# Moving six subtractions from GpSimd to VectorE in the first norm of a two-layer model, with an earlier weight load, one reordered subtraction per step and a 32-byte pad less

## The chip, the cores and the metric

The kernel runs on one core of a Trainium2 chip. A time is the device time of one execution in microseconds (us), and a kernel's time is the median of its runs. One further execution was taken under the hardware profiler; all durations of single instructions come from that one.

## The reference

The model has two layers over 512 tokens of width 1024. Each layer is a mixer (layer 0 a gated linear recurrence, layer 1 attention) followed by a mixture of 16384 small experts; each of these four parts is preceded by a norm whose scale and shift come from a vector `c` by a matrix:

```
def ada_modulation(c, w, b):
    mod = jax.nn.silu(c) @ w + b
    shift, scale, gate = jnp.split(mod, 3, axis=-1)

shift, scale, gate = ada_modulation(c, mw, mb)
h = rms_norm(x, g) * (1.0 + scale) + shift
x = x + gate * mixer(h, *mixer_params[layer])
```

The change touches the very first of the four norms and the first products of the mixer behind it (`xb, gb = jnp.split(h @ in_w, 2, axis=-1)`).

## The kernel before, in words

Every large matrix product is made from a split into two float32r halves: `hi` is a rounded copy that ScalarE writes, `lo` is the raw value minus `hi`, a subtraction with two inputs in SBUF. Three TensorE products then stand for one: `hi*hi`, `hi*lo`, `lo*hi`. `split` (lines 226 to 228) does this for weights, with ScalarE on line 227 and, on line 228, VectorE or, while the stream's `on_pool` is set, GpSimd.

`Stream` (line 128) feeds the weights of the whole program in the order in which they are used. `fetch` allocates a raw buffer (two of 1 MB, a block pair each) and issues its load on SyncE's DMA queue, `fill` splits blocks as far as asked, and `take` hands out one block.

`norm_first` (line 231) runs once, at the start of the program. It brings in the four token tiles of `x` and 16 rows of the modulation matrix (`mrow`, 512 KB each, a ring of 10), in the order scale row 8, shift row 0, then 9, 1, 10, 2 and so on; after every few rows it calls `g.stream.fetch()` for a pair of weight blocks. `normed_rows` scales each token tile (the `rs` power is a small GpSimd instruction) and TensorE transposes it into eight PSUM banks, one for each slice `k` of 128 channels. For each `k`:

- two `dot` calls: VectorE multiplies a row with `silu(c)` and sums it (line 278), ScalarE turns the sum into a column (lines 280, 283);
- ScalarE makes `hk = xt * scale + shift` (line 310) and its rounded copy `hhi` (line 311), VectorE subtracts `hlo = hk - hhi` (line 312);
- for `k` of 1 to 4 the next of four weight blocks is taken and split; at `k = 6` two more blocks are split ahead for the mixer;
- `products` issues the TensorE work that has become possible (lines 299 to 301): 4 blocks x 8 slices x 3 products, 96 in all.

Behind the norm, `lru` (line 530) reads the four finished blocks (ScalarE lines 613, 615, 625) and goes on with `proj_t` (lines 423 to 425), whose first PSUM bank is free when the `ge` activation of line 625 has read its block.

Each engine works through its own instructions strictly in the order in which they stand. That order is chosen by the scheduler of the language layer; an instruction wrapped in `tc.keep_in_program_order` keeps its place among others so wrapped. A DMA queue belongs to the engine that issues on it: a DMA that has to wait for a buffer holds up all later ones of the same engine.

Of the kernel before, what the change touches and what calls it, by code (L numbers as in the profile page):

```python
# [18 lines left out]
KD = D // 128  # L19
# [43 lines left out]
def setup(tc, ctx, g, x, c, out):  # L63
# [24 lines left out]
    nc.vector.memset(g.mhalf, -0.5)  # L88
    pad(g, g.const, 32)
    g.order = range(TC)  # L90
# [37 lines left out]
class Stream:  # L128
# [3 lines left out]
    def __init__(self, g, items, ahead=3):  # L132
# [5 lines left out]
        self.on_pool = False  # L138
        self.fetched = 0
        self.spare = None  # L140

    def fetch(self):

        (src, shape, n), b = self.blocks[len(self.parts)]
        self.loads += 1
        raw, bufs = self.g.wraw, 2
        if self.third and self.loads % 3 == 0:
            raw, bufs = self.third
        self.raw = raw.tile([128, n, *shape], F32, name="wraw", tag="wraw", bufs=bufs)
        self.g.nc.sync.dma_start(self.raw, src)  # L150
        self.fetched = self.loads

    def fill(self, last):
# [3 lines left out]
        while len(self.parts) <= last:  # L157
            (src, shape, n), b = self.blocks[len(self.parts)]
            if b == 0:
                if not self.fetched:  # L160
                    self.fetch()
                self.fetched = 0
            raw = self.raw[:, b]
# [67 lines left out]
def norm_first(g, mwT, sub):  # L231
# [8 lines left out]
    with pool(tc, name="mw0", bufs=10) as mw, pool(tc, name="nw", bufs=2) as nw, \  # L240
# [7 lines left out]
        def loads():  # L248
# [8 lines left out]
            for k in range(1, KD):  # L257
                fetch(KD + k)
                fetch(k)
                if k in (2, 4):  # L260
                    yield
                    g.stream.fetch()
# [12 lines left out]
        def dot(r):  # L275
            wf = rows.pop(r).rearrange("p a b -> p (a b)")
            d = nw.tile([128, 1], F32, name="dot", tag="dot", bufs=4)
            V.scalar_tensor_tensor(wf, wf, 1.0, g.sc, op0=OP.mult, op1=OP.mult, accum_out=d)
            if r < KD:
# [22 lines left out]

        for k in range(KD):
            if k:
                dot(KD + k)
                dot(k)
            if k in (1, 3):
                next(moved)
            hk = nw.tile([128, S], F32, name="hk", tag="hk")
            A.activation(hk, xt[k], AF.Identity, scale=cols[KD + k], bias=cols[k])  # L310
            A.activation(hhi[:, k, :], hk, AF.Copy)
            V.tensor_sub(hlo[:, k, :], hk, hhi[:, k, :])
            if 1 <= k <= m:
                g.stream.on_pool = True
                g.stream.spare = nw if k <= 2 else None
                w.append(g.stream.take(0))
                g.stream.on_pool = False
            if k == KD - 2:
                g.stream.on_pool = True
                g.stream.fill(m + 1)  # L320
                g.stream.on_pool = False
            if k:
# [1152 lines left out]
```

## Time and profile before

| | us |
|---|---|
| median of 3 runs | 3165.71 (3160.58 to 3170.85) |
| profiled execution, its own time | 3167.8 |
| its span in the trace | 3166.0 |
| TensorE (PE) busy | 3061.6 |
| VectorE (DVE) busy | 2556.2 |
| ScalarE (ACT) busy | 1468.7 |
| GpSimd (POOL) busy | 1000.5 |

In a line of the timeline view the columns are the start and the duration in us, the engine, the source line, the operation, what it writes and reads, the count of merged instructions, and in brackets the idle time ahead of it and what ended that. SPq is SyncE's DMA queue; PEld is TensorE's weight load. Instructions of one engine overlap a little, so the distance between two starts is what one costs its engine, somewhat less than its duration.

### The profile page before, as it was taken

The numbers are of one execution on the slowest core, as the hardware profiler recorded it, in microseconds if no ns is written. First come the engines' busy times: TensorE is split into PE (matmuls) and PEld (weight loads), VectorE is DVE, ScalarE is ACT, GpSimd is POOL, SyncE is SP. The second block draws the span as 40 slices with busy tenths as digits, with TensorE's granted clock in tenths as the row PEclk, the third lists the DMA queues.
The fourth block names the chain that finished last, engine by engine and source line by source line (L and its number), as shares of the span: only waits on it lengthen the run. The fifth ranks groups of instructions, "written<-read, shape, count | busy, mean of one in ns | idle before, by whom it ended". The sixth has DMA issues, their size and how long they took to land.

```text
span 3166.0 us, 44376 instructions
## 1 busy us (share of the span) xinstructions
PE 3061.6 (97%) x16192; PEld 2686.4 (85%) x16192; DVE 2556.2 (81%) x5260; ACT 1468.7 (46%) x2129; POOL 1000.5 (32%) x859
## 2 busy tenths in 40 slices
PE   6998999999999999999899999999999999999999
PEld 5876999998788888888777778999987888888887
DVE  7866779977988888887579976789968888888884
ACT  5763337873333333333458744257853333333332
POOL 3001540007545246552011103420036454544430
PEclk9998999999999999999999999999999999999999
DMA  6545344789999999997332243345799999999983
GB/s 262 167 174 168 114 146 145 271 295 393 370 372 349 376 358 357 363 351 264 125 118 94 82 147 119 121 148 212 270 353 384 353 371 336 350 335 350 355 314 117
DMA packets 304780, 818.98 MB, mean 259 GB/s; under 512 B 27824, under 2 KB 156848, under 8 KB 276016
## 3 DMA queue, kind: packets, MB, share of 16 engines
q1 hardware_dynamic: 173680, 391.93, 35.5%
q0 software_dynamic: 89408, 321.43, 27.1%
q10 hardware_dynamic: 41472, 102.78, 8.7%
q8 instruction: 127, 2.08, 0.3%
q14 instruction: 93, 0.76, 0.1%
HBM read 735.03 MB, written 81.02 MB: 258 GB/s over the span
## 4 chain that ended last, share of the span: by engine, by line
PE 71%; DVE 15%; DMA 5%; ACT 4%; issue 4%; POOL 1%; SPq 0%; DVEq 0%; ACTq 0%; POOLq 0%
PE vacc L1038 28%; PE pacc L425 11%; PE pacc L423 11%; PE pacc L424 11%; DVE wlo L228 3%; DVE pg L929 2%; DMA wraw<-in_l_v_dram 2%; DMA wraw<-in_l_uT_dram 1%; DVE rows L953 1%; PE gps L905 1%; DVE p L921 1%; DVE p L918 1%; DVE ge L816 1%; DMA at<-ascr 1%; ACT whi L227 1%
## 5 line engine op out<-in xcount | busy, mean ns | idle before, releaser
L227 ACT ACTIVATE whi<-wraw 128x1024 fp32r<-128x1024 f32 (+2 forms) x646 | 663.3, 1034 | 651.2 <-PE pacc L424 392.3
L423 PE MATMUL pacc<-hhi,whi 128*128 128x384 f32 (+1 forms) x2616 | 922.1, 352 | 10.6 <-ACT whi L227 6.6
L425 PE MATMUL pacc<-hhi,wlo 128*128 128x384 f32 (+1 forms) x2616 | 918.5, 351 | 7.7 <-DVE wlo L228 7.7
L424 PE MATMUL pacc<-hlo,whi 128*128 128x384 f32 (+1 forms) x2616 | 916.9, 350 | 0.0
L228 DVE TENSOR_TENSOR wlo<-wraw,whi 128x1024 fp32r<-128x1024 f32 (+1 forms) x566 | 683.1, 1210 | 184.4 <-ACT whi L227 184.0
L1038 PE MATMUL vacc<-wlo,wh 128*128 128x512 f32 x1536 | 605.8, 394 | 1.1 <-DVE wlo L228 1.1
L1038 PE MATMUL vacc<-whi,wh 128*128 128x512 f32 x1536 | 602.7, 392 | 2.2 <-ACT whi L227 2.2
L1038 PE MATMUL vacc<-whi,wl 128*128 128x512 f32 x1536 | 597.2, 389 | 4.9 <-DVE wl L1031 4.9
L423 PEld LDWEIGHTS pacc<-hhi,whi 128*128 128x128 f32 x2616 | 494.6, 189 | 41.3 <-ACT whi L227 7.4
L425 PEld LDWEIGHTS pacc<-hhi,wlo 128*128 128x128 f32 x2616 | 494.0, 189 | 34.8 <-DVE wlo L228 10.8
L424 PEld LDWEIGHTS pacc<-hlo,whi 128*128 128x128 f32 x2616 | 494.7, 189 | 28.8 <-issue 1.7
L1028 ACT ACTIVATE wh<-at 128x384 fp32r<-128x384 f32 x256 | 134.1, 525 | 790.4 <-DVE at L1024 532.0
L944 POOL DMA_INDIRECT rows<-in_l_v_dram,ei x256 | 361.6, 1412 | 382.4 <-DVE accg L965 342.7
L944 POOL DMA_INDIRECT rows<-in_l_u_dram,ei x256 | 370.8, 1449 | 282.7 <-DVE rows L953 230.6
L1038 PEld LDWEIGHTS vacc<-whi,wl 128*128 128x128 f32 x1536 | 288.7, 188 | 70.5 <-DVE wl L1031 6.1
L1038 PEld LDWEIGHTS vacc<-whi,wh 128*128 128x128 f32 x1536 | 288.6, 188 | 64.2 <-ACT whi L227 2.6
L1038 PEld LDWEIGHTS vacc<-wlo,wh 128*128 128x128 f32 x1536 | 289.0, 188 | 54.2 <-DVE wlo L228 1.8
L965 DVE SCALAR_TENSOR_TENSOR accg<-rows,act,accg 128x1024 f32<-128x1024 f32 x254 | 324.7, 1278 | 0.5
L953 DVE SCALAR_TENSOR_TENSOR rows<-rows,hn 128x1024 f32<-128x1024 f32 x256 | 304.8, 1220 | 15.0 <-DMA rows<-in_l_u_dram,ei 15.0
L1024 DVE TENSOR_TENSOR at<-at,gtile 128x384 f32<-128x384 f32 x256 | 140.9, 553 | 147.7 <-DMA at<-ascr 141.4
L228 POOL TENSOR_TENSOR wlo<-wraw,whi 128x1024 fp32r<-128x1024 f32 (+1 forms) x80 | 171.5, 2155 | 226.9 <-ACT whi L227 226.9
L907 ACT ACTIVATE st<-gps 128x512 f32<-128x512 f32 x192 | 184.5, 1110 | 39.0 <-PE gps L905 38.8
(295 smaller groups left out, 3401.1 us busy)
## 6 DMA issues: line engine op xcount, KB each, us to landing
wraw<-in_l_uT_dram SPq DMA_DIRECT2D x128, 1024.0 KB, 7.0
wraw<-in_l_v_dram SPq DMA_DIRECT2D x128, 1024.0 KB, 9.9
gscr<-st ACTq DMA_DIRECT2D x48, 1024.0 KB, 4.6
gtile<-gscr SPq DMA_DIRECT2D x32, 1536.0 KB, 16.9
mw<-in_l_ffn_mw_dram POOLq DMA_DIRECT2D x48, 512.0 KB, 3.6
ascr<-at ACTq DMA_DIRECT2D x112, 192.0 KB, 2.7
at<-ascr ACTq DMA_DIRECT2D x112, 192.0 KB, 8.3
mw<-in_l_mix_mw_dram POOLq DMA_DIRECT2D x32, 512.0 KB, 6.5
```

The costliest lines, as they stand in the source:

```text
L227: g.nc.scalar.activation(hi, raw, AF.Copy)
L228: (eng or g.nc.vector).tensor_sub(lo, raw, hi)
L423: nc.tensor.matmul(ps, whi[:, k, :], hhi[:, k, :n], start=(k == 0), stop=False)
L424: nc.tensor.matmul(ps, whi[:, k, :], hlo[:, k, :n], start=False, stop=False)
L425: nc.tensor.matmul(ps, wlo[:, k, :], hhi[:, k, :n], start=False, stop=(k == KD - 1))
L907: A.activation(st[:, :, q * 4:q * 4 + 4].rearrange("p e t -> p t e"), gps, AF.Copy, scale=1.0 / GSCALE)
L944: i = nc.gpsimd.indirect_dma_start(out=rows, out_offset=None, in_=src, in_offset=bass.IndirectOffsetOnAxis(ap=ei[:, j:j + 1], axis=0))
L953: V.scalar_tensor_tensor(r, r, 1.0, hn, op0=OP.mult, op1=OP.mult, accum_out=act[:, j:j + 1]))
L965: tc.keep_in_program_order(V.scalar_tensor_tensor(acc, r, w, acc, op0=OP.mult, op1=OP.add))
L1024: pin(V.tensor_tensor(at.rearrange("p (b t) -> p b t", t=16), at.rearrange("p (b t) -> p b t", t=16), gts[c // 8][:, :, c % 8, :], op=OP.m ...
L1028: pin(A.activation(wh, at, AF.Copy))
L1038: T.matmul(acc[t][d], x[:, ts], y[:, d, :], start=(i == 0 and x is wh and y is vh), stop=(i == PK - 1 and x is wl))
```

## The change

Five edits, all in the first norm, its stream helper and the setup:

1. The six low halves of weights that the first norm splits go from GpSimd to VectorE.
2. The two pairs of weight blocks are asked for after modulation rows 1 and 3 instead of 2 and 4. `fetch` may now run ahead of blocks that are not split yet.
3. `finish(k)` issues `hk` and `hhi` and returns the subtraction for `hlo`; it is issued after the dots of slice `k + 1`.
4. The dots and the `hlo` subtractions are kept in program order.
5. A pad of 32 bytes per partition in the constants is removed, with its GpSimd memset. Every tile that is allocated behind it on the left side of SBUF starts 32 bytes lower; the tiles of `x`, on the right side, stay.

```
-    pad(g, g.const, 32)
@@ Stream
-        self.fetched = 0
+        self.next = None
...
-        (src, shape, n), b = self.blocks[len(self.parts)]
+        (src, shape, n), b = next(x for x in self.blocks[len(self.parts):] if x[1] == 0)
...
-        self.raw = raw.tile([128, n, *shape], F32, name="wraw", tag="wraw", bufs=bufs)
-        self.g.nc.sync.dma_start(self.raw, src)
-        self.fetched = self.loads
+        self.next = raw.tile([128, n, *shape], F32, name="wraw", tag="wraw", bufs=bufs)
+        self.g.nc.sync.dma_start(self.next, src)
...
-                if not self.fetched:
+                if self.next is None:
                     self.fetch()
-                self.fetched = 0
+                self.raw, self.next = self.next, None
@@ norm_first
-                if k in (2, 4):
+                if k in (1, 3):
                     yield
                     g.stream.fetch()
...
-            V.scalar_tensor_tensor(wf, wf, 1.0, g.sc, op0=OP.mult, op1=OP.mult, accum_out=d)
+            tc.keep_in_program_order(
+                V.scalar_tensor_tensor(wf, wf, 1.0, g.sc, op0=OP.mult, op1=OP.mult, accum_out=d))
...
-        for k in range(KD):
-            if k:
-                dot(KD + k)
-                dot(k)
-            if k in (1, 3):
-                next(moved)
+        def finish(k):
             hk = nw.tile([128, S], F32, name="hk", tag="hk")
             A.activation(hk, xt[k], AF.Identity, scale=cols[KD + k], bias=cols[k])
             A.activation(hhi[:, k, :], hk, AF.Copy)
-            V.tensor_sub(hlo[:, k, :], hk, hhi[:, k, :])
+            return lambda: tc.keep_in_program_order(V.tensor_sub(hlo[:, k, :], hk, hhi[:, k, :]))
+
+        for k in range(KD):
+            if k in (0, 2):
+                next(moved)
+            low = finish(k)
+            if k + 1 < KD:
+                dot(KD + k + 1)
+                dot(k + 1)
+            low()
             if 1 <= k <= m:
-                g.stream.on_pool = True
                 g.stream.spare = nw if k <= 2 else None
                 w.append(g.stream.take(0))
-                g.stream.on_pool = False
             if k == KD - 2:
-                g.stream.on_pool = True
                 g.stream.fill(m + 1)
-                g.stream.on_pool = False
```

What this makes of the order of instructions is shown at three places. Behind the first norm, the rows of all engines are the same in both programs, apart from line numbers and one load of gate weights on SyncE's queue, which now stands ahead of the three small loads `cv`, `gbias` and `lm` of the mixer, not behind them.

The first place is VectorE from the third token tile's `rs` on (`xn` is a scaled token tile, `mrow,dot` a dot, `wlo` the low half of a weight block). Before:

```order
L344 TENSOR_SCALAR ms<-ss 128x1
L278 SCALAR_TENSOR_TENSOR mrow,dot<-mrow,sc 128x1024
L348 TENSOR_SCALAR xn<-x_199,rs 128x512 x2
L278 SCALAR_TENSOR_TENSOR mrow,dot<-mrow,sc 128x1024 x2
L312 TENSOR_TENSOR hlo<-hk,hhi 128x512 x2
L278 SCALAR_TENSOR_TENSOR mrow,dot<-mrow,sc 128x1024
L312 TENSOR_TENSOR hlo<-hk,hhi 128x512
L278 SCALAR_TENSOR_TENSOR mrow,dot<-mrow,sc 128x1024 x3
```

And in the changed program:

```order
L343 TENSOR_SCALAR ms<-ss 128x1
L347 TENSOR_SCALAR xn<-x_197,rs 128x512 x2
L277 SCALAR_TENSOR_TENSOR mrow,dot<-mrow,sc 128x1024 x2
L306 TENSOR_TENSOR hlo<-hk,hhi 128x512
L226 TENSOR_TENSOR wlo<-wraw,whi 128x1024
L277 SCALAR_TENSOR_TENSOR mrow,dot<-mrow,sc 128x1024 x2
L306 TENSOR_TENSOR hlo<-hk,hhi 128x512
L277 SCALAR_TENSOR_TENSOR mrow,dot<-mrow,sc 128x1024
L226 TENSOR_TENSOR wlo<-wraw,whi 128x1024
```

One dot has moved from ahead of the last token tile to behind it, and the first low half of a weight stands between the first `hlo` and the dots of slice 2.

The second place is VectorE at the end of the first norm. Before:

```order
L278 SCALAR_TENSOR_TENSOR mrow,dot<-mrow,sc 128x1024 x3
L312 TENSOR_TENSOR hlo<-hk,hhi 128x512
L278 SCALAR_TENSOR_TENSOR mrow,dot<-mrow,sc 128x1024 x3
L312 TENSOR_TENSOR hlo<-hk,hhi 128x512 x2
L612 MEMSET xp 128x3 x2
```

And in the changed program:

```order
L277 SCALAR_TENSOR_TENSOR mrow,dot<-mrow,sc 128x1024 x2
L306 TENSOR_TENSOR hlo<-hk,hhi 128x512
L226 TENSOR_TENSOR wlo<-wraw,whi 128x1024 x2
L306 TENSOR_TENSOR hlo<-hk,hhi 128x512
L611 MEMSET xp 128x3 x2
```

The two low halves for the mixer's next blocks now stand ahead of the last `hlo`.

The third place is GpSimd from its constants to the mixer (`mw` is a modulation row that the mixer's background work reads). Before:

```order
L96 IOTA ji 128x128
L56 MEMSET pad 128x8
L96 IOTA ji 128x128
L346 TENSOR_TENSOR rs<-ms,mhalf 128x1 x4
L228 TENSOR_TENSOR wlo<-wraw,whi 128x1024 x6
L185 DMA mw<-in_l_mix_mw_dram 128x1024 x8
```

And in the changed program:

```order
L1470 UNCONDITIONAL_BRANCH
L95 ISA
L95 IOTA ji 128x128 x2
L345 TENSOR_TENSOR rs<-ms,mhalf 128x1 x4
L183 DMA mw<-in_l_mix_mw_dram 128x1024 x8
```

The first `mw` loads stand directly behind the last `rs`; the first two of them wait for nothing else.

## The prediction

> **What bounds the kernel now.** I read the page's busy times and its chain first, then the windows view, to see where TensorE has slack at all.
>
> ```profile
> PE 3061.6 (97%) x16192; PEld 2686.4 (85%) x16192; DVE 2556.2 (81%) x5260; ACT 1468.7 (46%) x2129; POOL 1000.5 (32%) x859
> PE 71%; DVE 15%; DMA 5%; ACT 4%; issue 4%; POOL 1%; SPq 0%; DVEq 0%; ACTq 0%; POOLq 0%
> 0.00:58.00 58.00, 34.09 (x130) 25.17 (x131) 37.24 (x59) 32.27 (x60) 22.69 (x18) 1.00 0.66 253
> 800.00:1200.00 400.00, 394.75 (x1906) 348.22 (x1906) 343.78 (x523) 139.35 (x193) 186.72 (x147) 1.00 0.99 362
> 2500.00:2900.00 400.00, 400.00 (x1945) 353.81 (x1944) 329.21 (x427) 140.69 (x193) 190.88 (x135) 1.00 0.96 349
> ```
>
> In the last three lines the columns are the stretch, its length, the busy time of PE, PEld, DVE, ACT and POOL with counts, the granted clock, the DMA share and GB/s. TensorE works 97% of the span; it is idle for 104 us in all, and 24 of these lie in the first 58 us. This is the stage that the change edits; behind it the order of instructions is the same. So the question is one number: when does TensorE begin the mixer's first own product (line 423), now at 57.58? Whatever that start gains, the PE-bound rest passes on nearly whole.
>
> Next I read the timeline of that stage, engine by engine.
>
> ```profile
> 18.26 1.22 DVE L278 SCALAR_TENSOR_TENSOR mrow<-mrow,sc 128x1024 f32<-128x1024 f32 x1
> 26.37 6.35 POOL L228 TENSOR_TENSOR wlo<-wraw,whi 128x1024 fp32r<-128x1024 f32 x2 [8.94 <-ACT whi L227]
> 27.13 3.36 DVE L278 SCALAR_TENSOR_TENSOR mrow<-mrow,sc 128x1024 f32<-128x1024 f32 x1
> 39.15 3.37 DVE L278 SCALAR_TENSOR_TENSOR mrow<-mrow,sc 128x1024 f32<-128x1024 f32 x1
> 44.82 0.50 PE L301 MATMUL pacc<-hhi,wlo 128*128 128x512 f32 x1 [0.32 <-POOL wlo L228]
> 51.73 0.69 DVE L312 TENSOR_TENSOR hlo<-hk,hhi 128x512 fp32r<-128x512 f32 x1 [1.24 <-ACT hhi L311]
> 54.59 0.39 PE L301 MATMUL pacc<-hhi,wlo 128*128 128x512 f32 x1
> 55.02 0.60 ACT L613 ACTIVATE xp<-pacc 128x512 f32<-128x512 f32 x1 [1.43 <-PE pacc L301]
> 56.65 0.39 PE L301 MATMUL pacc<-hhi,wlo 128*128 128x512 f32 x1
> 56.93 0.60 ACT L625 ACTIVATE ge<-pacc 128x512 f32<-128x512 f32 x1
> 57.58 0.50 PE L423 MATMUL pacc<-hhi,whi 128*128 128x512 f32 x1 [0.54 <-ACT ge L625]
> ```
>
> A dot takes 1.22 us alone; the two shown beside GpSimd's subtractions, and the two that follow them, take 3.4: two-input instructions of the two engines hold each other up. VectorE is done with the last `hlo` at 52.4, but TensorE still works off a backlog until 57.0, because the low half of the fourth block came only at 44.82. So two things end the stage: VectorE's queue, and behind it TensorE's backlog.
>
> **The change, part by part.** *Taken away:* four dots cost 3.37 - 1.22 = 2.15 us less each, 8.6 us of VectorE.
>
> *Added:* six low halves of weights on VectorE. The nearest row is the same instruction in the mixer; the dots' starts show what one of that size costs its engine.
>
> ```profile
> 74.79 1.22 DVE L228 TENSOR_TENSOR wlo<-wraw,whi 128x1024 fp32r<-128x1024 f32 x1
> 45.77 0.68 DVE L312 TENSOR_TENSOR hlo<-hk,hhi 128x512 fp32r<-128x512 f32 x1
> 46.38 1.21 DVE L278 SCALAR_TENSOR_TENSOR mrow<-mrow,sc 128x1024 f32<-128x1024 f32 x1
> 47.52 1.21 DVE L278 SCALAR_TENSOR_TENSOR mrow<-mrow,sc 128x1024 f32<-128x1024 f32 x1
> ```
>
> From 46.38 to 47.52 is 1.14 for a dot, and the same for a low half of a weight; from 45.77 to 46.38 is 0.61 for an `hlo`. Six low halves are 6.8 us.
>
> *Moved dot:* row 9's dot goes behind the last token tile, 1.14 more for later. In return no dot stands beside the second and fourth `rs`.
>
> ```profile
> 9.60 0.57 POOL L346 TENSOR_TENSOR rs<-ms,mhalf 128x1 f32<-128x1 f32 x1 [1.53 <-DVE ms L344]
> 11.29 1.46 POOL L346 TENSOR_TENSOR rs<-ms,mhalf 128x1 f32<-128x1 f32 x1 [1.12 <-DVE ms L344]
> ```
>
> The second shrinks from 1.46 to about 0.57, and the fourth alike. Row 0's dot and the column behind it now stand behind the second token tile and hold up the third tile's squares on ScalarE by about 1.5 us, so I set the start of the dots behind the last tile at 18.26 as before (bounds 17.4, if only the `rs` gain counts, and 19.4).
>
> *New waits:* now VectorE itself waits for ScalarE's `whi`, in order, ahead of its next dots. What ScalarE needs from a dot's end I take from these rows.
>
> ```profile
> 48.67 1.22 DVE L278 SCALAR_TENSOR_TENSOR mrow<-mrow,sc 128x1024 f32<-128x1024 f32 x1
> 50.25 0.78 ACT L310 ACTIVATE hk<-xt,col_l_mix,col_l_mix 128x512 f32<-128x512 f32 x1
> 51.06 0.63 ACT L311 ACTIVATE hhi<-hk 128x512 fp32r<-128x512 f32 x1
> 51.60 1.99 ACT L227 ACTIVATE whi<-wraw 128x1024 fp32r<-128x1024 f32 x2
> 52.72 4.74 POOL L228 TENSOR_TENSOR wlo<-wraw,whi 128x1024 fp32r<-128x1024 f32 x2 [7.96 <-ACT whi L227]
> ```
>
> The dot ends at 48.67 + 1.14 = 49.81, the reader of `whi` starts at 52.72: 2.91 us. The first low half stands behind dots 9 and 1 with only an `hlo` (0.61) between: VectorE stands idle for 2.3. The second has an `hlo` and a dot more in front and waits for nothing. The third's `whi` goes ahead of `hhi` on ScalarE, so 2.91 less 51.60 - 51.06 = 0.54, which is 2.37, less 0.61, idle for 1.76. The fourth waits for nothing. The fifth stands behind the last dot: 2.3 again, and the last `hlo` is queued behind it and the sixth.
>
> *VectorE's sum* from 18.26: 14 dots 16.0, eight `hlo` 4.9, six low halves 6.8, idle 2.3 + 1.76 + 2.3. It ends at 52.3, where before it ended at 52.4. What the lock gives back, the new work and the new waits eat.
>
> *TensorE behind it:* here lies the gain. The low halves of weights come in time, so no backlog is left; after the last `hlo` (start 51.7) eight products remain. A product can start 0.75 after its `hlo` started, and one costs 0.23:
>
> ```profile
> 37.39 0.69 DVE L312 TENSOR_TENSOR hlo<-hk,hhi 128x512 fp32r<-128x512 f32 x1 [1.83 <-ACT hhi L311]
> 38.14 0.50 PE L300 MATMUL pacc<-hlo,whi 128*128 128x512 f32 x1
> 29.46 0.80 PE L301 MATMUL pacc<-hhi,wlo 128*128 128x512 f32 x1 [1.90 <-POOL wlo L228]
> 31.33 0.63 PE L299 MATMUL pacc<-hhi,whi 128*128 128x512 f32 x1
> 31.76 0.63 PE L300 MATMUL pacc<-hlo,whi 128*128 128x512 f32 x1
> 33.37 0.39 PE L300 MATMUL pacc<-hlo,whi 128*128 128x512 f32 x1
> 33.60 0.39 PE L301 MATMUL pacc<-hhi,wlo 128*128 128x512 f32 x1
> ```
>
> Block 0 gets its last product at 51.7 + 0.75 + 0.23 = 52.7; `xp` reads it 0.43 later (54.59 to 55.02 above), `ge` follows 1.91 later with a table load between, and line 423 0.65 after `ge` started: 55.7. TensorE begins 1.9 us earlier. If all three idle times were hidden, it would begin 6.4 earlier still.
>
> *Loads.* The rows' supply is no bound:
>
> ```profile
> L246 SPq DMA_DIRECT2D mrow<-in_l_mix_mw_dram x16: 327/328/654, 2.1 to 24.3; - x16
> DMA to landing us min/median/max: 4.2/11.4/12.6
> 29.00:32.70 3.70, 2.93 (x6) 1.00 1.03 409
> 57.41 1.27 POOL L185 DMA_DIRECT2D mw<-in_l_mix_mw_dram  x2
> 45.22 0.38 SPq L539 DMA_DIRECT2D cv<-in_lru_conv_dram  x1
> gbias<-in_lru_bias_dram SPq DMA_DIRECT2D x1, 11.0 KB, 4.0
> ```
>
> The last row is asked for at 24.3 and lands by 36.9 at the latest; its dot comes at 45.6. Asking for weights two rows sooner delays rows by 2.5 us that are not needed yet, and TensorE could not start on the weights before `hhi` anyway: zero, covered by VectorE's queue. GpSimd is free from 18 us, so the two `mw` loads go out then and not at 57.41; 1 MB at 409 GB/s delays the rows by 2.6, again ahead of need. `cv` now stands behind a load that waits for the sixth low half (51.9) and is issued at 52.4 instead of 45.22. If it takes the 4.0 of `gbias` (in the last line of the fence, the median from issue to landing), it lands at 56.4, under a microsecond after ScalarE could use it; TensorE has a block of 24 products (5.5 us) before it needs what follows. Zero, with 0.8 as its price without that cover.
>
> *The pad.* No row prices it; its memset is 0.1 us at the start of GpSimd, beside VectorE's wait for the first rows. For the 32 bytes I take zero, and bound them among the rivals.
>
> **Sum.** The profiled execution took 3167.8 (span 3166.0 and 1.8 around it); 1.9 less is 3165.9. Its own time stands 2.1 above the median of the runs, so against 3165.7 I expect **3163.8 us**, no change within 0.3% (9.5 us), about what a measurement of this kernel can tell from none.
>
> **The rivals.** *The waits are shorter than I make them.* For it: ScalarE is 46% busy and the scheduler may have chosen this order because its `whi` come early. Against: in the order shown `whi` stands behind that slice's column, `hk` and `hhi`. All idle time gone: 3163.8 - 6.4 = 3157.4.
>
> *TensorE stays at half rate.* Until 32 us its products start 0.43 apart, then 0.23, at a granted clock that the view shows as 1.00 throughout. The faster rate came after a dense run from 29.46. In the new order products come in short groups, each waiting on VectorE, so the dense run may come late. At 0.43 all the way, 96 products from 23.5 last until 64.8, and line 423 starts 7.2 later than now: 3173. It decides only if the change comes after about 40 us, since until then VectorE is the slower one. Against it: at 0.43 the groups themselves become dense, which brings the faster rate. The Trainium skill ("TensorE: Matmul & The Clock Gate", Part 1) says that the array is throttled to half until about 3.4 us of sustained activity; the trace agrees (29.46 to about 33), and by that rule the half rate would end soon after the groups close up, and cost little.
>
> *The pad makes loads slower.* In the 400 us from 800 and the 400 from 2500 the DMA share is 0.96 to 0.99 at about 355 GB/s, and TensorE idles 5.3 us there in all. If tiles that start 32 bytes lower made these loads longer by 1%, that slack would be gone and the kernel 8 - 5.3 = 2.7 us slower; from 2% on it is 11 and more: 3175 and up. If loads got faster, TensorE could gain 5.3 at most there: 3158.5. Against both: load pieces start at multiples of 32 bytes before and after, and 409 GB/s was reached in the first stage at one such offset. The Trainium skill ("DMA: Bandwidth & Descriptors", How a descriptor splits into AXI transactions) charges a piece for the bytes between its start and the 256-byte boundary below; by that rule lower offsets (96 to 64, 32 to 0) save one beat of 32 bytes in some 130 to 260, under 1%, on the fast side.
>
> *The change does not free VectorE*, since GpSimd keeps other work beside the dots. Only the two `mw` issues (1.27 us) are left there, so hardly: 3166.
>
> **How the numbers follow.** Forecast 0.62 (own range 3160 to 3168), shorter waits 0.12, half rate 0.11, pad slower 0.07, pad faster 0.05, nothing freed 0.03. Faster by over 0.3% means below 3156.2: half of the pad's and a third of the shorter waits' cases, with the runs' own scatter of 5 us either way, 0.12. Slower, above 3175.2: the pad's and a little of the half rate, 0.09. Same 0.79. The range goes from 3154 to 3174.
>
> **What would show it.** All 16 dots near 1.22; VectorE idle for about 2 us ahead of the first, third and fifth `wlo`, each put down to ACT `whi`; its last `hlo` ending at 52 +- 1.5; line 423 at 55.7; `mw` issued near 18 us. I am wrong if line 423 starts before 53 or after 58, or if any stretch behind 100 us changes its length by over 3 us.

## The result, and the profile after

The changed kernel is faster: 3146.68 us (median of 6 runs, 3143.22 to 3148.86) against 3169.79 for the kernel before beside it, a ratio of 0.9931 with a 95% interval of 0.9917 to 0.9945. By the ratio that is 22 us (the two medians lie 23.1 apart); 1.9 us were forecast, which the prediction counted as no change. Run again later, beside other kernels, it gave 0.9940 (0.9926 to 0.9955). Its profiled execution took 3146.06 with a span of 3144.2.

The page of the changed kernel, busy times and chain:

```profile
PE 3057.6 (97%) x16192; PEld 2684.4 (85%) x16192; DVE 2554.4 (81%) x5266; ACT 1468.8 (47%) x2129; POOL 980.2 (31%) x852
PE 71%; DVE 15%; DMA 5%; issue 5%; ACT 3%; POOL 0%; SPq 0%; DVEq 0%; ACTq 0%; POOLq 0%
```

Nothing here names a culprit: the shares are the same as before to a per cent, the 5% of DMA too. TensorE is idle for 86.6 us instead of 104.4, and busy for 4.0 less.

**The first norm** came out as worked out. From the timeline of the changed kernel:

```profile
11.79 0.48 PE L288 MATMUL pacc<-ident,xn 128*128 128x128 f32 x1 [11.79 <-DVE xn L347]
18.59 1.25 POOL L183 DMA_DIRECT2D mw<-in_l_mix_mw_dram  x2
24.58 1.22 DVE L226 TENSOR_TENSOR wlo<-wraw,whi 128x1024 fp32r<-128x1024 f32 x1 [2.18 <-ACT whi L225]
34.24 1.23 DVE L226 TENSOR_TENSOR wlo<-wraw,whi 128x1024 fp32r<-128x1024 f32 x1 [1.51 <-ACT whi L225]
47.49 0.69 DVE L306 TENSOR_TENSOR hlo<-hk,hhi 128x512 fp32r<-128x512 f32 x1
50.36 2.36 DVE L226 TENSOR_TENSOR wlo<-wraw,whi 128x1024 fp32r<-128x1024 f32 x2 [2.18 <-ACT whi L225]
52.63 0.68 DVE L306 TENSOR_TENSOR hlo<-hk,hhi 128x512 fp32r<-128x512 f32 x1
55.10 0.40 PE L300 MATMUL pacc<-hhi,wlo 128*128 128x512 f32 x1
56.05 0.60 ACT L624 ACTIVATE ge<-pacc 128x512 f32<-128x512 f32 x1
56.70 0.50 PE L422 MATMUL pacc<-hhi,whi 128*128 128x512 f32 x1 [1.21 <-ACT ge L624]
```

VectorE waits for `whi` ahead of the first, third and fifth low half, and the mixer's own first product (now line 422) starts at 56.70. In this execution everything started late: the first transpose came at 11.79, where in the kernel before it came here:

```profile
10.75 0.69 PE L289 MATMUL pacc<-ident,xn 128*128 128x128 f32 x2 [10.75 <-DVE xn L348]
```

Counted from the first transpose, the norm went from 57.58 - 10.75 = 46.83 to 56.70 - 11.79 = 44.91. The late start is of the execution, not of the change: in all the other traced executions of kernels with the changed first norm it lies between 10.51 and 11.49.

**The other 20 us** lie far behind the first norm. The engines' orders are the same there, so the same TensorE instruction can be found in both traces. How much earlier (-) it starts than in the kernel before, in us, by its start there (worked out from the trace's instruction records):

```
start before:               672    915   1396   2298   2484   3146
changed kernel             -1.2   -9.1   -9.5  -12.1  -21.8  -21.8
```

So 7.8 us come between 672 and 915, and 9.6 between 2298 and 2484; the other 4.3 us are spread over the rest. Both are starts of the same stage, one in each layer: the down phase of the experts. There TensorE multiplies the scaled first products (`wh`, `wl`) with the halves of a weight (`vacc` on line 1038, 1037 after; the first of them at 720 and at 2345 us in the kernel before), and at the same time GpSimd gathers 512 KB row tiles (`rows`) by an indirect DMA, SyncE loads 1 MB raw weights and the gates (`gtile`, 1.5 MB, from a scratch buffer in DRAM), and ScalarE's queue loads the first products (`at`). These tiles lie in two pools, opened one behind the other:

```
        with pool(tc, name="vw", bufs=2) as vw, ...:
            gguard = pool(tc, name="gat", bufs=8)
            gat = gguard.__enter__()
            pad(g, vw, 384)
            g.stream.third = (vw, 2)
            ...
                gts[n] = vw.tile([128, NB, 8, 16], F32, name="gtile", tag="gtile")
                ins[c] = vw.tile([128, ND], F32, name="at2", tag="at2", bufs=AHEAD + 2)
                wh = vw.tile([128, ND], F32R, name="wh", tag="wh", bufs=5)
                rows = env["gat"].tile([128, D], F32, name="rows", tag="gat")
```

With the 32-byte pad in the constants all of these start at 32 modulo 256 (the main raw weights and their halves at 96), without it at 0 (and at 64). The windows view, columns as in the prediction, of the kernel before:

```profile
700.00:860.00 160.00, 148.86 (x719) 131.62 (x718) 127.18 (x196) 50.52 (x74) 95.83 (x66) 0.98 1.03 382
2300.00:2480.00 180.00, 167.93 (x913) 151.01 (x913) 140.08 (x203) 72.00 (x98) 88.98 (x62) 0.97 1.00 371
```

and of the changed kernel, with the stretches that the prediction looked at below them:

```profile
700.00:860.00 160.00, 154.43 (x757) 137.70 (x756) 135.36 (x211) 53.79 (x77) 101.90 (x71) 0.99 1.03 399
2300.00:2480.00 180.00, 176.11 (x896) 157.37 (x896) 147.86 (x222) 69.86 (x97) 99.21 (x70) 0.99 1.02 396
0.00:58.00 58.00, 35.85 (x134) 26.66 (x135) 36.11 (x66) 33.28 (x63) 4.12 (x12) 0.94 0.76 291
800.00:1200.00 400.00, 398.23 (x1927) 352.04 (x1926) 345.43 (x521) 141.27 (x196) 188.49 (x147) 1.00 0.99 367
2500.00:2900.00 400.00, 400.00 (x1939) 353.08 (x1938) 327.61 (x417) 142.26 (x195) 191.49 (x133) 1.00 0.95 347
```

In the two starts the DMA engines are busy all the time in both kernels (share 1.00 to 1.03), but they move 399 instead of 382 GB/s, and 396 instead of 371. TensorE's idle time there falls from 11.1 to 5.6 and from 12.1 to 3.9 us. The waits view for the second start, of the kernel before:

```profile
PE pacc L423 <- ACT whi L227: 6.4, 1, 6.4
PE gps L905 <- DVE p L918: 1.9, 1, 1.9
PE vacc L1038 <- DVE wl L1031: 1.7, 1, 1.7
```

and of the changed kernel:

```profile
PE gps L904 <- DVE p L917: 1.9, 1, 1.9
PE pacc L424 <- DVE wlo L226: 0.2, 1, 0.2
```

(Columns: who waits for whom, us in total, times, the longest.) The 6.4 us in which TensorE stood for one late weight are gone. The view of the DMA transfers from 700 to 860 us shows what the traffic consists of, in the kernel before and then in the changed one:

```profile
DMA packets 26918, 61.14 MB, mean 382 GB/s; under 512 B 1513, under 2 KB 14825, under 8 KB 26017
gtile<-gscr SPq DMA_DIRECT2D x5, 1536.0 KB, 19.5
```

```profile
DMA packets 28404, 63.90 MB, mean 399 GB/s; under 512 B 1568, under 2 KB 15690, under 8 KB 27552
```

Over half of the packets (pieces, below) are small; by the trace's packet records 12288 of the 26918 are pieces of 512 bytes, and these are the gates; most of the others are pieces of 4 KB, rows and raw weights.

### The profile page after: what moved, and what is told of

The parts are those of the page before. It is cut to its first block, busy times and chain, and to the rows that moved or that the text cites. A ratio compares the mean times of both kernels' runs of the same rounds, so it can differ in the third digit from the quotient of the medians.

```text
span 3144.2 us, 44373 instructions
## 1 busy us (share of the span) xinstructions
PE 3057.6 (97%) x16192; PEld 2684.4 (85%) x16192; DVE 2554.4 (81%) x5266; ACT 1468.8 (47%) x2129; POOL 980.2 (31%) x852
## 4 chain that ended last, share of the span: by engine, by line
PE 71%; DVE 15%; DMA 5%; issue 5%; ACT 3%; POOL 0%; SPq 0%; DVEq 0%; ACTq 0%; POOLq 0%
PE vacc L1037 29%; PE pacc L422 11%; PE pacc L424 11%; PE pacc L423 11%; DVE wlo L226 3%; DMA wraw<-in_l_v_dram 2%; DVE rows L952 2%; DVE pg L928 2%; PE gps L904 1%; DVE p L920 1%; DMA mrow<-in_l_mix_mw_dram 1%; DVE p L917 1%; DVE ge L815 1%; PE oacc L464 1%; PE oacc L465 1%
## 5 line engine op out<-in xcount | busy, mean ns | idle before, releaser
L226 DVE TENSOR_TENSOR wlo<-wraw,whi 128x1024 fp32r<-128x1024 f32 (+2 forms) x572 | 690.9, 1211 | 192.0 <-ACT whi L225 189.5
L1037 PEld LDWEIGHTS vacc<-wlo,wh 128*128 128x128 f32 x1536 | 288.8, 188 | 53.3 <-DVE wlo L226 0.9
L226 POOL TENSOR_TENSOR wlo<-wraw,whi 128x1024 fp32r<-128x1024 f32 (+1 forms) x74 | 153.9, 2090 | 204.6 <-ACT whi L225 204.6
```

Source lines behind the costliest of these rows:

```text
L226: (eng or g.nc.vector).tensor_sub(lo, raw, hi)
L1037: T.matmul(acc[t][d], x[:, ts], y[:, d, :], start=(i == 0 and x is wh and y is vh), stop=(i == PK - 1 and x is wl))
```

## The experiments

Theory A: the 32 bytes, through the offsets of the tiles. Theory B, the rival: the edits of the first norm set another phase of the transfers, and the offsets do nothing. All ratios are against the kernel before on the same chip, with their 95% intervals.

### The pad alone, from both sides

```diff
+    pad(g, g.const, 32)        # changed kernel, at its old place
```

> The changed kernel with the 32-byte pad put back and nothing else undone. Theory A (tiles that start 32 bytes past a multiple of 64 make the transfers of the two DMA-bound starts of the down phases slower, 382 against 399 GB/s in the stretch from 700 to 860 us): nearly all of the gain goes, the time is 1 to 3 us below the kernel before (ratio 0.999), about 380 GB/s in that stretch. Theory B (the edits of the first norm set another phase of the transfers, and the offsets do nothing): it keeps the changed kernel's gain of 22 us, ratio 0.993, about 399 GB/s.

Measured: 0.9987 (0.9975 to 0.9999).

```diff
-    pad(g, g.const, 32)        # kernel before
```

> The kernel before with the 32-byte pad taken out and nothing else. Theory A (offset of the tiles): 18 to 22 us below the kernel before, ratio 0.993 to 0.994, about 399 GB/s from 700 to 860 us, with a first norm as long as before. Theory B (first norm's edits): as the kernel before, ratio 1.000, about 382 GB/s.

Measured: 0.9953 (0.9937 to 0.9969). The windows view of the first kernel, then of the second:

```profile
700.00:860.00 160.00, 153.28 (x745) 135.77 (x743) 131.47 (x205) 52.29 (x75) 98.36 (x68) 0.98 1.03 387
2300.00:2480.00 180.00, 168.20 (x883) 151.01 (x882) 139.73 (x207) 67.47 (x94) 93.11 (x66) 0.96 1.00 374
```

```profile
700.00:860.00 160.00, 157.35 (x773) 140.58 (x772) 136.79 (x211) 54.87 (x80) 101.80 (x71) 0.99 1.03 401
2300.00:2480.00 180.00, 174.45 (x872) 156.39 (x872) 142.73 (x216) 66.07 (x92) 96.70 (x69) 0.98 1.01 388
```

The rate of the transfers and most of the time go with the pad; theory B falls. With the pad the edits of the first norm leave 4 us (0.3 to 8). Without them the pad gives 15 us, 18 to 22 having been expected, and its interval reaches to 20. Counted from the first transpose, the mixer's first product starts after 44.92 us in the first kernel and 46.88 in the second: the edits' 1.95 us belong to them, and do not depend on the pad.

### Which tiles: the down phase's pools apart from the rest

```diff
-            pad(g, vw, 384)        # changed kernel
+            pad(g, vw, 416)
```

> The changed kernel with the pad of the down phase's pool grown from 384 to 416 bytes: only the tiles of that pool and the one above it (gathered rows, gates, first products, every third raw weight) start 32 bytes past a multiple of 64 again, the other raw weights and everything outside the down phases stay on multiples of 64. Theory A with the gathered rows, gates and first products as the cause: the gain goes, ratio 0.998 to 1.000. Theory A with the main raw weights as the cause: most of the gain stays, ratio 0.993 to 0.995; halfway if all transfers count alike (these tiles take about two thirds of the bytes there): 0.997. Theory B: 0.993.

Measured: 1.0029 (1.0018 to 1.0040), slower than the kernel before, which no theory had.

```diff
+    pad(g, g.const, 32)        # changed kernel
...
-            pad(g, vw, 384)
+            pad(g, vw, 352)
```

> The counterpart: the changed kernel with the 32-byte pad put back, and the pad of the down phase's pool cut from 384 to 352 bytes, so that only the tiles of that pool and the one above it start at multiples of 64, and all else 32 bytes past one, as before. Gathered rows, gates and first products as the cause: gain stays, 0.993 to 0.994. Main raw weights as the cause: gone, 0.999. All transfers alike: 0.995. Theory B: 0.993.

Measured: 0.9985 (0.9976 to 0.9994). Taken by the ratios alone, this says that both the down tiles and the main raw weights have to be even (to start at a multiple of 64; odd is 32 bytes past one). The traces say otherwise. The windows view of the first of the two, then of the second:

```profile
700.00:860.00 160.00, 148.78 (x710) 129.91 (x709) 125.44 (x194) 49.51 (x71) 94.98 (x66) 0.98 1.02 377
860.00:1400.00 540.00, 540.00 (x2589) 471.09 (x2588) 455.47 (x615) 189.85 (x261) 247.62 (x191) 1.00 0.99 358
```

```profile
700.00:860.00 160.00, 154.79 (x752) 136.40 (x751) 133.17 (x206) 52.42 (x75) 101.71 (x70) 0.99 1.01 394
860.00:1400.00 540.00, 540.00 (x2590) 471.40 (x2589) 457.74 (x613) 190.75 (x261) 248.20 (x192) 1.00 0.97 358
```

and of the changed kernel for the second stretch:

```profile
860.00:1400.00 540.00, 539.89 (x2623) 477.23 (x2622) 460.07 (x614) 190.71 (x262) 249.98 (x193) 1.00 0.98 360
```

In the start the rate follows the down tiles: 377 where they are odd, 394 where they are even. But from 860 on, where TensorE never waits, both kernels get only 2589 and 2590 products done in 540 us where the changed one does 2623: each product takes 1.3% longer, at the same granted clock of 1.00. My edits had moved the two operands of the down products against each other. Start to start, the median of the three kinds of down product is 229, 232 and 226 ns in the kernels before and after (`whi` with `wh`, `wlo` with `wh`, `whi` with `wl`), 234, 233 and 234 in the first of these two and 231, 232 and 237 in the second. At 1536 products a kind that is some 20 us. So the down tiles are the cause of the rate, the main raw weights are not, and a second effect, of the same size and not thought of, lies on top.

### Rows, gates, first products, third raw weights: one at a time

From here on the offset between the products' operands was left alone.

```diff
             pad(g, vw, 384)        # changed kernel
+            pad(g, gat, 32)
```

> The changed kernel with 32 bytes of padding in the pool of the gathered rows alone: the rows (and the modulation rows of the next norm, which use the same buffers) start 32 bytes past a multiple of 64, the gates, first products and all raw weights stay on multiples of 64, and the offset between the down products' two operands is unchanged. If the gathered rows are the cause: the gain goes, ratio 0.998 to 1.000, 375 to 387 GB/s from 700 to 860 us. If the gates, first products or third raw weights are: 0.993 and about 399 GB/s. If the earlier halves of the result were chance of the executions: anything from 0.993 to 1.000 without a change of the rate.

Measured: 0.9952 (0.9938 to 0.9966), 396 GB/s.

```diff
+    pad(g, g.const, 32)        # changed kernel
...
             pad(g, vw, 384)
+            pad(g, gat, 32)
```

> The counterpart: the changed kernel with the 32-byte pad back at its old place, and 32 bytes of padding in the pool of the gathered rows, so that these alone start at a multiple of 64 and every other tile 32 bytes past one, as before. Gathered rows as the cause: gain back, ratio 0.993 to 0.994 and 395 to 400 GB/s from 700 to 860 us. Gates, first products or third raw weights: 0.999, 380 to 387 GB/s.

The rows started at 64 here, a multiple of 64 but not of 256. Measured: 0.9988 (0.9975 to 1.0001), 388 GB/s: nothing came back.

```diff
+                if n == 0:         # changed kernel, around the first gate tile
+                    nc.gpsimd.memset(vw.tile([128, 8], F32, name="padb", bufs=1), 0.0)
                 gts[n] = vw.tile([128, NB, 8, 16], F32, name="gtile", tag="gtile")
+                if n == 0:
+                    nc.gpsimd.memset(vw.tile([128, 56], F32, name="padc", bufs=1), 0.0)
```

> So far 394 to 401 GB/s from 700 to 860 us came in just those kernels whose down-phase pool starts at 0 modulo 256, and 377 to 388 where it starts at 32, 64 or 128; the rows' own offset did little. Here, in the changed kernel, the gates alone (moved in pieces of 512 bytes, about half of all packets there) start at 32 modulo 256, everything else in that pool and the rows at 0. Theory C (512-byte pieces that do not start at a multiple of 256 slow the transfers beside them): the gain goes, 377 to 388 GB/s, ratio 0.997 to 1.000. Theory D (the first products, the scaled products or every third raw weight): 394 to 401 GB/s, ratio 0.993 to 0.995.

Measured: 0.9951 (0.9937 to 0.9965). The rate in the profiled execution was 397 GB/s, so it speaks against theory C, while the time does for a part of it.

The opposite, with the pad in the constants back, 224 bytes ahead of the gates and 32 behind them:

> The counterpart: the 32-byte pad back, every tile at its offset of before modulo 256, and the gates alone at 0 modulo 256. Theory C (512-byte pieces): gain back, 394 to 401 GB/s from 700 to 860 us, ratio 0.993 to 0.995. Theory D: 382 to 388 GB/s, 0.998 to 1.000.

Measured: 0.9950 (0.9937 to 0.9963), 391 GB/s. The gates alone bring back some 70% of what the pad takes (0.9987 to 0.9936).

The same two pads of 32 and 224 bytes around the first products instead, in the changed kernel:

> The changed kernel with only the first products of the down phase's pool (pieces of 1536 bytes, 3% of the bytes from 700 to 860 us) at 32 modulo 256. If each tile costs as its own pieces do: hardly anything, since the pieces took 65 to 67 ns wherever they stood: as the changed kernel, 0.993, 395 to 400 GB/s. If these tiles are what makes the others' packets slow: 0.996 to 0.998, below 390 GB/s.

Measured: 0.9938 (0.9922 to 0.9955). And around the two buffers for every third raw weight:

> The changed kernel with only every third raw weight of the down phase (two buffers of 8 KB) at 32 modulo 256. If each tile costs by its own pieces: pieces of 4 and 8 KB went from 159 and 309 ns to 164 and 315 in the kernels with the slow rate, 2 to 3% on about a tenth of the bytes there: 0.3% of the rate, 0.993 to 0.994, 396 to 399 GB/s. If these tiles are what is missing beside rows and gates: 0.995 to 0.996, below 393 GB/s.

Measured: 0.9930 (0.9916 to 0.9945). Neither costs anything that can be measured; the third of this set was the changed kernel itself:

> The changed kernel itself, on the same chip as the three others: 0.993 of the kernel before.

Measured: 0.9940 (0.9926 to 0.9955).

Rows alone and gates alone cost some 5 us each (0.9952 and 0.9951 against 0.9936, the mean of the changed kernel's two; the intervals overlap, so neither is clear of noise by itself). Do the two together make up the whole? The gates and rows at 32 and all else at 0:

> The changed kernel with the gates and the rows at 32 modulo 256 and all else of the down phase at 0. If the two are the whole cause: 0.998 to 0.999 as with the pad back, 380 to 388 GB/s from 700 to 860 us, gate pieces at 30 ns and the rows' pieces of 4 KB at a median of 164 ns. If they only add up to 12 us: 0.997, about 392 GB/s, rows at 159 to 162 ns.

Measured: 0.9978 (0.9968 to 0.9989). And with the pad in the constants back, the gates and rows alone at 0:

> The changed kernel with the 32-byte pad back, and the gates and the rows alone at 0 modulo 256. If the two are the whole cause: 0.993 to 0.994, 394 to 401 GB/s, rows' pieces at 159 ns. If the gates alone do what can be had (0.995 with them alone at 0): 0.995 again.

Measured: 0.9928 (0.9913 to 0.9942). The windows view of the first and of the second:

```profile
700.00:860.00 160.00, 151.98 (x728) 134.47 (x727) 130.60 (x202) 52.29 (x75) 99.16 (x68) 0.97 1.03 388
```

```profile
700.00:860.00 160.00, 155.44 (x762) 138.58 (x761) 136.43 (x211) 55.09 (x79) 105.49 (x71) 0.99 1.03 400
```

These two tiles are the cause, within the intervals whole and alone: the second kernel has the pad, has every other tile at its start of before modulo 256, and is as fast as the changed kernel; the first loses as much as the pad takes, less 3 us that its interval covers.

### Multiples of 64, or of 256?

```diff
+    pad(g, g.const, 64)        # changed kernel
```

> The changed kernel with a pad of 64 bytes where the one of 32 stood: every tile behind it starts 64 bytes higher, still at a multiple of 64, and no tile stands where it stands in the changed kernel. If a multiple of 64 is what counts: as the changed kernel, 0.993 and 395 to 400 GB/s. If low offsets above a 256-byte boundary count (rows at 64 instead of 0, raw weights at 128 instead of 64): slower than the kernel before, whose rows stood at 32: 1.000 to 1.003. If 0 modulo 256 for the rows counts: 0.997 to 1.000.

Measured: 0.9994 (0.9983 to 1.0005). A multiple of 64 does nothing.

```diff
-            pad(g, vw, 384)        # changed kernel
+            pad(g, vw, 256)
```

> The changed kernel with the pad of the down phase's pool cut from 384 to 256 bytes: that pool's tiles and the rows start at 128 modulo 256 instead of 0, on multiples of 64, and the scaled products stand 64 bytes above the weights' offset instead of 64 below. If multiples of 64 are what counts for the transfers, about 399 GB/s from 700 to 860 us again. On the products of the down phase (start to start 229, 232 and 226 ns now, 234, 233 and 234 where the down tiles alone stood 32 higher): if the offset between their operands modulo 64 decides, 229/232/226 and 0.993; if its exact size does, other times, each ns worth 1536 ns a group, between 678 (three times 226, ratio 0.989) and 701 ns for the three (0.999).

Measured: 1.0047 (1.0030 to 1.0064), with the products at 233 ns each. The windows view of the first, and of the second:

```profile
700.00:860.00 160.00, 150.59 (x736) 133.31 (x735) 128.77 (x198) 52.38 (x76) 96.41 (x67) 0.99 1.02 385
```

```profile
700.00:860.00 160.00, 153.23 (x741) 134.10 (x740) 130.28 (x202) 53.16 (x77) 97.54 (x68) 0.99 1.03 387
```

At 64 and at 128 the rate is as low as at 32. All the runs together, from 700 to 860 us (packet times from the trace's packet records; a star where the products' offset was changed too):

```
                       start mod 256   gates, 512 B   rows, 4 KB    rate   ratio
                       gates  rows     mean ns        median ns     GB/s
changed kernel            0     0       27.4           159           399   0.9931
pad gone alone            0     0       27.4           159           401   0.9953
only down tiles even      0     0       27.5           159           394   0.9985 *
weights at 128            0     0       27.1           159           405   0.9982 *
weights at 0              0     0       27.3           159           403   0.9919 *
first products odd        0     0       27.2           159           398   0.9938
third raw odd             0     0       27.2           159           403   0.9930
changed again             0     0       27.2           159           392   0.9940
layout, norm before       0     0       27.2           159           401   0.9927 *
gates and rows even       0     0       27.3           159           400   0.9928
rows odd                  0    32       27.1           159           396   0.9952
gates even                0    32       27.1           159           391   0.9950
gates odd                32     0       29.6           159           397   0.9951
rows even                32    64       30.3           164           388   0.9988
kernel before            32    32       30.0           164           382   1
pad back                 32    32       30.0           164           387   0.9987
only down tiles odd      32    32       30.1           164           377   1.0029 *
gates and rows odd       32    32       30.0           162           388   0.9978
all 64 higher            64    64       29.9           164           385   0.9994
down tiles at 128       128   128       30.5           162           387   1.0047 *
```

On the mean a gate piece takes 27 ns where it starts at a multiple of 256 and 30 elsewhere, whatever else is moved. It is not that each takes 3 ns more: in the kernel before 53% of the pieces take 27 ns or less and nearly all others 28 to 41, in the changed one 99% take 27. The rows' median goes up only where both stand badly. It is not the rows alone that slow down then: with gates and rows odd, the raw weights' pieces of 4 KB, whose own starts are those of the changed kernel, go from a median of 159 to 161 ns.

An estimate from the packet records of the kernels before and after shows which pieces make up the rate. The differences of the mean times (30.0 against 27.4 ns for 512 bytes, 167.5 against 162.3 for 4 KB, 332 against 317 for 8 KB), times the counts of the kernel before from 700 to 860 us, give 104 us, or 6.5 on each of 16 engines: 4% of the stretch, about what the rate gains (382 to 399). A third of it is in the gates' own pieces, over half in those of 4 KB.

By the middle values, rows or gates alone cost some 5 us and the two together 13 to 19 (0.9978 against 0.9936, and 0.9987 against 0.9928), more than their sum; at the ends of the intervals it is 10, their sum, so the times alone do not show this.

### The products' offset, and a faster version

```diff
+    pad(g, g.const, 64)        # changed kernel
...
-            pad(g, vw, 384)
+            pad(g, vw, 320)
```

> The changed kernel with 64 bytes more ahead of the weights' pool and 64 bytes less ahead of the down phase's: that pool stays at 0 modulo 256, the weights' halves start at 128 instead of 64, 128 above the scaled products modulo 256. The transfers should keep 394 to 401 GB/s. Down products, start to start, in the order whi with wh, wlo with wh, whi with wl: with a difference of 64 they took 229, 232, 226 ns; of 96: 231, 232, 237; of 32 and of 192: 234, 233, 234. If the difference modulo 64 decides, 192 should have been as good as 64, and it was not; so the size of the difference does, and here it is open: 678 to 702 ns for the three, 3144 to 3161 us minus or plus: ratio 0.989 (226 each) to 0.999 (234 each).

Measured: 0.9982 (0.9971 to 0.9992). With 192 bytes at both places instead:

> As the run with the weights at 128, but with 192 bytes more ahead of the weights' pool and 192 less ahead of the down phase's, so that both start at 0 modulo 256, a difference of 0. Transfers: 394 to 401 GB/s. Down products: 678 to 702 ns for the three; the projections of the same stretch, whose operands both stand in the weights' pool and the one of h, at a difference of 0 all the time, take 173 to 174 ns for 384 columns, so a difference of 0 may be a good one: ratio 0.989 if the products take 226 each, 0.999 if 234 each.

Measured: 0.9919 (0.9904 to 0.9935), 3138.79 us. The windows view of this one, in the stretch where TensorE does not wait:

```profile
860.00:1400.00 540.00, 540.00 (x2630) 478.65 (x2629) 463.17 (x617) 190.33 (x261) 250.73 (x195) 1.00 0.98 362
```

2630 products in place of 2623. The medians, start to start, by how far the weights' halves start above the scaled products, modulo 256 (means leave out distances over 300 ns):

```
weights above products     whi,wh   wlo,wh   whi,wl    (ns)
   0  weights at 0            227      227      227     (means 226.8, 228.1, 228.6)
  32  only down tiles odd     234      233      234
  64  before, changed         229      232      226     (means 229.2, 231.6, 226.0)
  96  only down tiles even    231      232      237
 128  weights at 128          231      231      232
 192  down tiles at 128       233      233      233
```

The three numbers at 64 are the same where the halves and the scaled products start at 96 and 32, at 64 and 0, and at 128 and 64 (the run with all 64 higher), so there it is the difference that counts. For the other differences there is one pair of starts each.

An estimate from the means settles the two runs whose ratios misled above. At 96 the three take 699.9 ns instead of 686.8 (231.4, 231.7 and 236.8), which at 1536 of each is 20 us, so without it "only down tiles even" would stand at 0.992 instead of 0.9985. At 32 they take 699.4 (233.5, 232.9 and 233.0), 19 us, so "only down tiles odd" would stand at 0.997 instead of 1.0029, near the 0.9978 of the run with gates and rows odd.

The last experiment on it puts the first norm of before into this layout:

```diff
-    pad(g, g.const, 32)        # kernel before
+    pad(g, g.const, 192)
...
-            pad(g, vw, 384)
+            pad(g, vw, 192)
```

> The kernel before with its own first norm, but with the layout of the run with the weights at 0 (192 bytes ahead of the weights' pool, 192 ahead of the down phase's). That layout with the changed first norm gave 0.9919. If the first norm's edits are worth the 2.4 us that the trace shows at 190 us: 0.9925 to 0.993. If they are worth 7 us (the changed kernel's 0.9931 against 0.9953 with the pad gone alone): 0.994.

Measured: 0.9927 (0.9913 to 0.9940). The layout does nearly all of it, and between 0.9919 and 0.9927 lie the 2 to 3 us of the first norm, too little for these intervals to show by themselves. Is the layout with the weights at 0 better than the changed kernel? Its products are, by the means by 3 ns in 687, which is some 5 us in all; its ratio (0.9919) stands below both of the changed kernel's (0.9931 and 0.9940), but the intervals overlap, and the two were not run side by side.

## Why the prediction was wrong

**What held: the first norm.** The forecast gain was 1.9 us; from the first transpose to the mixer's first product it is 46.83 - 44.91 = 1.92, and between 44.89 and 44.92 in all 17 traced kernels with the changed norm. The dots behind the last token tile take 1.21 to 1.22. VectorE's idle times were forecast at 2.3, 1.76 and 2.3 and are 2.18, 1.51 and 2.18. Its last `hlo` ends at 53.3, at 52.3 with the late start taken out, as forecast. The `mw` loads are issued at 18.59, as forecast. The last product of block 0's backlog is gone: after the last `hlo` there are eight products. Line 422 was forecast at 55.7; 56.70 less the late start of 1.04 is 55.66. The rival of shorter waits did not come: the three idle times are together 0.5 us shorter than forecast, not 6.4. That the end fits to 0.1 us is in part luck, since the dots behind the last token tile began 0.14 later than forecast (19.44 less 1.04 is 18.40) and the work between, with its small gaps, took some 0.3 more.

**Half rate** to the end did not come either, and for the reason given against it. From the timeline of the changed kernel:

```profile
31.37 0.62 PE L298 MATMUL pacc<-hhi,whi 128*128 128x512 f32 x1
31.79 0.63 PE L299 MATMUL pacc<-hlo,whi 128*128 128x512 f32 x1
34.35 0.59 PE L300 MATMUL pacc<-hhi,wlo 128*128 128x512 f32 x1
34.78 0.39 PE L298 MATMUL pacc<-hhi,whi 128*128 128x512 f32 x1
35.01 0.40 PE L299 MATMUL pacc<-hlo,whi 128*128 128x512 f32 x1
```

The clock that this trace shows as granted is 0.50 from 24.53 to 27.95, 1.00 until 31.36, 0.50 again until 34.77 and 1.00 from there. So TensorE had the full rate once and lost it, after a stretch of short groups in which it was busy for 1.56 of 3.41 us. At 0.42 the products then close up into a dense run from 31.37; from 34.78 on they are 0.23 apart. That is 3.4 us later. The Trainium skill's figure for the warm-up ("TensorE: Matmul & The Clock Gate", Part 1) is 3.4 us: the trace agrees. In the kernel before the trace has no record of the clock ahead of 32.85, so the 1.00 that the prediction read for its first stage says nothing of the products 0.43 apart.

**What failed: "For the 32 bytes I take zero".** The pad is worth 15 us alone (0.9953) and 16 beside the other edits (from 0.9987 to the mean of the changed kernel's two, 0.9936). The price that the rival "if loads got faster" gave it, 5.3 us at most, was wrong by its window. It was the idle time of TensorE in the 400 us from 800 and the 400 from 2500. The first down products come at 720 and 2345, and it is in these starts (the stretches from 700 and from 2300), with the DMA share at 1.00 to 1.03, that TensorE was idle, 11.1 us and 12.1. Two rows of the windows view for these stretches would have made the bound 23 us, and a range that reaches to it holds the result. The 5% that the chain gives to DMA I passed over, since the first norm alone seemed to hold TensorE's slack; they could not have sized the gain, being 5% after the change as well.

**The evidence against the pad was taken from the wrong transfers.** The 409 GB/s at one such offset in the first stage are loads in pieces of 4 KB, apart from a few of 4 bytes; there are no pieces of 512 bytes in it. The Trainium skill's rule ("DMA: Bandwidth & Descriptors", How a descriptor splits into AXI transactions) has the boundary right: in these runs what counts is the 256-byte one, since 64 and 128 are as bad as 32. I applied it to the large pieces only, "some 130 to 260" beats. A gate piece of 512 bytes is 16 beats; by an estimate from the rule it needs 17 from an offset of 32, 18 from 64 and 20 from 128, or 6, 12 and 25% more. Measured are means of 30.0, 29.9 and 30.5 ns against 27.4, or 9 to 11% at any of the three, and about half of the pieces take no longer at all: the rule names the right pieces, but the grading by beats does not show. For the rows the same estimate gives 1 beat in 128, under 1%. Their mean in the two kernels is 167.4 against 161.9 ns, 3%; whether they wait for the gates is not shown.

**The test in the prediction fired.** "Any stretch behind 100 us changes its length by over 3 us" was named as the sign of error, and the two starts changed by 7.8 and 9.6.

What stays open: why rows and gates at bad offsets seem to cost more together than apart (13 to 19 us against 5 and 5 by the middle values), and why only half of the gate pieces slow down. A path that both share and on which both are slowed would explain the first, but no run here looks into that. Nor was it tried what in the products depends on the offset between their operands.

## What to carry to other kernels

Price a change of memory layout in the stretches where the DMA engines are saturated, not on the average: find them by a DMA share of 1.0 in narrow windows, and take TensorE's whole idle time there as the bound. Start tiles that receive many small pieces, and those that are filled beside them, at a multiple of 256 bytes; an edit that drops a small pad shifts every tile behind it, and that can outweigh everything else that it does. When a layout experiment comes out worse than all theories, compare the stretch in which nothing waits: an edit meant for the transfers may have slowed the instructions.

## What the runs showed of the hardware

- The start of the gates and rows modulo 256 bytes decides the DMA rate under saturation here: 391 to 405 GB/s with the gates at a multiple of 256 and 377 to 388 in all kernels but one with them elsewhere (the one has 397, with only the gates off). Starts at 32, 64 and 128 are alike; none other was tried. It is worth 0.5% of this kernel.
- TensorE's products depend on where their two operands stand against each other: 226 to 237 ns, start to start, for the same instruction of 512 columns at the same clock, 687 ns for the three kinds at a difference of 64 modulo 256, 681 at 0 (by the means 684), up to 701 at 32 (by the means 699). At 1536 of each kind that is some 20 us from 64 to 32, an estimate, about as much as the whole change.
- The granted clock of TensorE fell to half for 3.41 us after a stretch of 3.41 us in which it was busy for 1.56, and came back after as long a dense run.
